# Where the operands of the weight products begin in an SBUF partition: from 704 bytes past a multiple of 2 KB to the multiple itself

## Chip, cores, metric

One Trainium2 chip, one core of it. The metric is device time in microseconds (us) of one execution; the kernel before takes 1866.35 us, the median of 3 runs (1865.23 to 1867.15).

## What is computed

One decoder layer on 256 tokens of width 2048, everything in float32:

```python
h = x + 0.5 * swiglu(rms_norm(x), w_gate1, w_up1, w_down1)        # 2048 -> 5632 -> 2048
proj = rms_norm(h) @ w_in                                          # q, k, v, forget logits; q, k, v
o = concat([rms_norm(forgetting_attention(...)),                   # 16 heads of 64, causal
            rms_norm(sliding_window_sink_attention(...))])         # 16 query, 4 key heads, window 128
h = h + o @ w_out
y = h + 0.5 * swiglu(rms_norm(h), w_gate2, w_up2, w_down2)
```

Nearly all of the arithmetic is in the eight weight matrices. Each is read once, 336 MB in all.

## The kernel before

**Products.** A weight product multiplies activations (stationary operand, 128 rows by 128 tokens) with a block of weights (moving operand, 128 rows by 512 columns) and adds into one PSUM bank. To keep float32 accuracy each operand is split into a high part of type float32r and the remainder, and `mm3` (L178 to L181) issues three matmuls for each product: high by high (L179), high by low weights (L180), low activations by high weights (L181). Every matmul loads its own stationary operand first.

**Loop.** `token_major` (L184) runs over the contraction in steps of two 128-row groups (`kg`, with `k` 0 and 1 in it) and over the two halves of 128 tokens. For each `kg` it calls `weights` (L90): SP issues the transfer of a tile `raw` of 128 by 1024 float32 (L93), ScalarE rounds it to `whi` (L94), VectorE subtracts to get `wlo` (L95). Each of the three has four buffers. `k` 0 takes the first `width` columns of `whi` and `wlo`, `k` 1 the next `width` (L195). `width` is 512, but 388 for the projection `ws` of the sliding-window part and the forget logits, whose tile is 776 wide.

**Stages.** FFN1 gate and up (11 blocks of 512 columns each, stationary operand `u`), FFN1 down (`hT`, 44 groups of 128, of the tile `hT1`), the 388-wide projection (`u`), attention together with the projections `wf` (`u`), the output projection (first half `u` buffers, second half `oTf`), FFN2 gate and up (`u`), FFN2 down (`hT2`). Between the products TensorE transposes results for the next stage (L213). PE, ACT and DVE work through lists whose order is fixed when the program is built.

**Places in SBUF.** Tiles of a pool lie one behind the other in a partition, in steps of 32 bytes, pool behind pool in the order `keep`, `wp`, `sp`, and then `f1`, `mix` and `f2` in the same place one after the other. `cst` (3712 bytes), `vec` (904) and `pos` (8) come first, then `h`, `u0` and `u1` (16,384 each) and the twelve weight tiles (4096 each), all sizes multiples of 2048; so all of these begin at the same remainder. The program built from the kernel has these starts, as remainders of the start in the partition by 2048 bytes:

| operand | role | start mod 2048 | bytes read by one matmul |
|---|---|---|---|
| `whi`, `wlo`, 512 wide, k 0 and 1 | moving | 704 | 2048 |
| `whi`, `wlo`, 388 wide, k 0 / k 1 | moving | 704 / 208 | 1552 |
| `u0`, `u1` | stationary | 704 (+ 0, 512, 1024, 1536 for part and token half) | 512 |
| `hT1`, `hT2` | stationary | 1184 (+ the same) | 512 |
| `oTf0`, `oTf1` | stationary | 640 (+ the same) | 512 |

A 512-wide moving operand so always runs across a multiple of 2 KB (704 + 2048 bytes). Of the 388-wide ones that of k 0 does (704 + 1552 = 2256), and that of k 1 doesn't (208 + 1552 = 1760). Of the stationary ones one in four does.

## Time and profile before

| | |
|---|---|
| median of 3 runs | 1866.35 us |
| the profiled execution, its own time | 1865.22 us |
| its span in the trace, first to last instruction | 1863.0 us |
| TensorE busy | 1834.8 us (98%) |
| weight loads busy (PEld) | 1513.8 us (81%) |
| VectorE / ScalarE busy | 986.2 us (53%) / 843.4 us (45%) |
| DMA, read from HBM | 336 MB, 182 GB/s over the span |
| mean granted TensorE clock | 0.995 |

Matmuls overlap in the trace: a 512-wide one is shown with 0.39 us while the next starts 0.23 us after it. What a stream of them costs is therefore read from the distance of their starts (called pace below), never from the duration. The timeline gives starts to 10 ns; a pace is taken over many starts.

### The profile page before, as it was taken

To read this page: it belongs to the slowest core of one execution; us is meant where nothing else is said; L and a number is where in the kernel's file an instruction comes from. 1 tells how busy PE (TensorE), PEld (TensorE's weight loads), DVE (VectorE), ACT (ScalarE), POOL (GpSimd) and SP (SyncE) were. 2 spreads that over 40 slices of the span, in tenths; PEclk is the share of its full clock that TensorE was granted. 3 is DMA by queue.
4 is the path that set the end of the run, shared out by engine and by line. 5 is a ranking of instruction groups with operands and counts; after the bars stand their busy time and mean duration, and the time that the engine had idled before them with its cause. 6 is when DMAs were issued, how large, how long until landed. Compare 5 with 4: busy or idle time off the path is not lost.

```text
span 1863.0 us, 21805 instructions
## 1 busy us (share of the span) xinstructions
PE 1834.8 (98%) x8396; PEld 1513.8 (81%) x8396; DVE 986.2 (53%) x1194; ACT 843.4 (45%) x1073; POOL 20.9 (1%) x27
## 2 busy tenths in 40 slices
PE   8999999999999999969999999999999999999999
PEld 6888888888888888967888788888888888888887
DVE  6445545454544444666757665454554554444443
ACT  6444444444434443535657554444444444433332
POOL 2000000000000000000000000000000000000000
PEclk9999999999999999989999999999999999999999
DMA  8555555555555555553444355555555555555553
GB/s 301 190 189 191 193 189 188 188 192 192 186 187 181 185 188 175 177 160 104 155 140 146 136 187 186 192 187 187 191 192 188 184 192 190 185 190 199 197 203 113
DMA packets 96440, 339.79 MB, mean 182 GB/s; under 512 B 10832, under 2 KB 10960, under 8 KB 96080
## 3 DMA queue, kind: packets, MB, share of 16 engines
q1 hardware_dynamic: 95040, 336.19, 52.3%
q10 hardware_dynamic: 1296, 2.21, 0.4%
q8 instruction: 65, 1.06, 0.2%
q14 instruction: 39, 0.32, 0.1%
HBM read 336.27 MB, written 2.10 MB: 182 GB/s over the span
## 4 chain that ended last, share of the span: by engine, by line
PE 97%; DMA 1%; DVE 1%; ACT 0%; issue 0%; SPq 0%; DVEq 0%; ACTq 0%
PE acc L179 31%; PE acc L181 31%; PE acc L180 31%; PE sm L213 1%; DMA xc<-in_xT 1%; PE sc L546 1%; PE sm L441 1%; PE sm L447 1%; PE sc L618 1%; PE sm L597 0%; DMA raw<-in_wg 0%; PE sm L448 0%; ACT whi L94 0%; DVE tr L516 0%; DVE qr L517 0%
## 5 line engine op out<-in xcount | busy, mean ns | idle before, releaser
L95 DVE TENSOR_TENSOR wlo<-raw,whi 128x1024 fp32r<-128x1024 f32 (+2 forms) x648 | 778.7, 1203 | 833.9 <-ACT whi L94 833.5
L94 ACT CAST whi<-raw 128x1024 fp32r<-128x1024 f32 (+2 forms) x648 | 667.1, 1031 | 910.3 <-PE acc L181 892.5
L179 PE MATMUL acc<-whi,u 128*128 128x512 f32 (+1 forms) x1792 | 693.3, 388 | 2.7 <-ACT u L152 2.2
L181 PE MATMUL acc<-whi,u 128*128 128x512 f32 (+1 forms) x1792 | 691.5, 387 | 2.5 <-DVE u L153 2.5
L180 PE MATMUL acc<-wlo,u 128*128 128x512 f32 (+1 forms) x1792 | 692.0, 386 | 0.7 <-DVE wlo L95 0.7
L179 PEld LDWEIGHTS acc<-whi,u 128*128 128x128 f32 x1792 | 336.3, 188 | 69.2 <-ACT u L152 2.6
L181 PEld LDWEIGHTS acc<-whi,u 128*128 128x128 f32 x1792 | 336.2, 188 | 68.6 <-DVE u L153 3.4
L180 PEld LDWEIGHTS acc<-wlo,u 128*128 128x128 f32 x1792 | 336.5, 188 | 66.0 <-DVE wlo L95 1.9
L179 PE MATMUL acc<-whi,hT 128*128 128x512 f32 x704 | 278.5, 396 | 0.0
L180 PE MATMUL acc<-wlo,hT 128*128 128x512 f32 x704 | 278.1, 395 | 0.0
L181 PE MATMUL acc<-whi,hT 128*128 128x512 f32 x704 | 278.0, 395 | 0.0
L181 PEld LDWEIGHTS acc<-whi,hT 128*128 128x128 f32 x704 | 131.9, 187 | 32.3
L180 PEld LDWEIGHTS acc<-wlo,hT 128*128 128x128 f32 x704 | 132.0, 187 | 32.1
L179 PEld LDWEIGHTS acc<-whi,hT 128*128 128x128 f32 x704 | 132.0, 187 | 32.0
L419 ACT ACTIVATE s<-s,nm 128x128 f32<-128x128 f32 (+1 forms) x64 | 28.3, 444 | 11.2 <-DVE nm L416 8.5
L222 DVE TENSOR_TENSOR hT<-sm,hT 128x512 fp32r<-128x512 f32 x44 | 28.2, 682 | 0.0
L179 PE MATMUL acc<-whi,oTf 128*128 128x512 f32 x64 | 25.3, 396 | 0.0
L180 PE MATMUL acc<-wlo,oTf 128*128 128x512 f32 x64 | 25.1, 391 | 0.0
L181 PE MATMUL acc<-whi,oTf 128*128 128x512 f32 x64 | 25.0, 391 | 0.0
L221 ACT CAST hT<-sm 128x512 fp32r<-128x512 f32 x44 | 23.5, 587 | 0.0
L213 PEld LDWEIGHTS sm<-cst,s 128*128 128x128 f32 x176 | 20.5, 140 | 2.9
L213 PE MATMUL sm<-cst,s 128*128 128x128 f32 x176 | 22.8, 272 | 0.0
(175 smaller groups left out, 568.2 us busy)
## 6 DMA issues: line engine op xcount, KB each, us to landing
raw<-in_wu SPq DMA_DIRECT2D x176, 512.0 KB, 3.2
raw<-in_wd SPq DMA_DIRECT2D x176, 512.0 KB, 3.2
raw<-in_wg SPq DMA_DIRECT2D x168, 512.0 KB, 3.2
raw<-in_wf SPq DMA_DIRECT2D x48, 512.0 KB, 3.6
raw<-in_wo SPq DMA_DIRECT2D x32, 512.0 KB, 3.5
raw<-in_ws SPq DMA_DIRECT2D x32, 388.0 KB, 3.5
raw<-in_wg SPq DMA_DIRECT2D x16, 256.0 KB, 5.2
xc<-in_xT SPq DMA_DIRECT2D x8, 256.0 KB, 4.9
```

What stands on the lines that cost most here:

```text
L94: nc.scalar.copy(hi, raw)
L95: nc.vector.tensor_tensor(out=lo, in0=raw, in1=hi.bitcast(F32), op=ALU.subtract)
L179: nc.tensor.matmul(o, lhsT=shi, rhs=mhi, start=start, stop=False)
L180: nc.tensor.matmul(o, lhsT=shi, rhs=mlo, start=False, stop=False)
L181: nc.tensor.matmul(o, lhsT=slo, rhs=mhi, start=False, stop=stop)
L213: nc.tensor.transpose(bt[:, j * SEQ + t * P : j * SEQ + (t + 1) * P], src[:, t, m], ident)
L221: nc.scalar.copy(hs[:, :, 0, :], v)
L222: nc.vector.tensor_tensor(out=hs[:, :, 1, :], in0=v, in1=hs[:, :, 0, :].bitcast(F32), op=ALU.subtract)
L419: nc.scalar.activation(s[:, j, :], s[:, j, :], AF.Exp, bias=nm[:, i, j : j + 1], accum_out=den[:, i, j : j + 1],)
L441: nc.tensor.transpose(bt[:, j * P : (j + 1) * P], src[:, j, :], ident)
L447: nc.tensor.matmul(bo[rows, c0 : c0 + SEQ], lhsT=vals(0, j), rhs=p0[:, j, :], start=True, stop=False)
L546: nc.tensor.matmul(o_, lhsT=qk[aa][:, j, blk * P : (blk + 1) * P], rhs=qk[aa][:, 4 + half, 0:nk], start=True, stop=True,)
```

## The change

Only places change. `vec` is widened to 1024 bytes and a filler `pad` of 1248 bytes is put behind `pos`, so that `h`, the `u` buffers and the weight tiles begin at multiples of 2048. A filler `sppad` of 1568 bytes makes the pool `sp` end at such a multiple too, so that `hT1` begins at one; a filler of 128 bytes in the pool `f2` puts `hT2` 128 bytes past one. `pf` and `nsink` are widened to 128 bytes each, which puts `oTf0` and `oTf1` at 1664 past one (13 times 128). The 388-wide tiles are loaded as two blocks with a stride of 512 columns, so that k 1 begins at a multiple too; transfer, cast and subtraction of these 32 tiles work on a pattern of 2 by 388 for it.

| operand | start mod 2048 before | after |
|---|---|---|
| `whi`, `wlo`, 512 wide | 704 | 0 |
| `whi`, `wlo`, 388 wide, k 0 / k 1 | 704 / 208 | 0 / 0 |
| `u0`, `u1` | 704 | 0 |
| `hT1` | 1184 | 0 |
| `hT2` | 1184 | 128 |
| `oTf0`, `oTf1` | 640 | 1664 |

No moving operand crosses a multiple of 2 KB any more. No instruction is added, taken away or moved: on each of the five engines the built programs have the same operations in the same order with the same waits; the 32 transfers, casts and subtractions of the 388-wide tiles differ in their pattern alone.

```diff
@@ -89,16 +89,24 @@
 
     def weights(src, tiles=None, at=0):
 
-        raw, hi, lo = (t[:, at : at + src.shape[1]] for t in tiles or weight_tiles())
+        tiles = tiles or weight_tiles()
+        if src.shape[1] % 512:
+            n = src.shape[1] // 2
+            raw, hi, lo = (t.rearrange("p (k n) -> p k n", k=2)[:, :, :n] for t in tiles)
+            src = src.rearrange("p (k n) -> p k n", k=2)
+        else:
+            raw, hi, lo = (t[:, at : at + src.shape[1]] for t in tiles)
         nc.sync.dma_start(raw, src)
         nc.scalar.copy(hi, raw)
         nc.vector.tensor_tensor(out=lo, in0=raw, in1=hi.bitcast(F32), op=ALU.subtract)
-        return hi, lo
+        return tiles[1:]
 
 
     cst = keep.tile([P, C_END], F32, name="cst")
-    vec = keep.tile([P, V_END], F32, name="vec")
+    vec = keep.tile([P, 256], F32, name="vec")
     pos = keep.tile([P, NT], I32, name="pos")
+
+    keep.tile([P, 312], F32, name="pad")
 
     h = keep.tile([P, NT, D], F32, name="h")
     ident = cst[:, C_ID : C_ID + P]
@@ -107,7 +115,7 @@
     m_swa = cst[:, C_MSK : C_MSK + SEQ]
     m_fox = cst[:, C_MSK + SEQ : C_MSK + 2 * SEQ]
     m_caus = m_fox[:, P:SEQ]
-    nc.scalar.dma_start(vec, a["vec"])
+    nc.scalar.dma_start(vec[:, :V_END], a["vec"])
 
     def half_u(i):
         return keep.tile([P, 8, 2, SEQ], F32R, tag="u%d" % i, name="u%d" % i, bufs=1)
@@ -192,7 +200,7 @@
             hi, lo = parts
             for k in range(2):
                 kk = kg * 2 + k
-                m = slice(k * width, (k + 1) * width)
+                m = slice(k * 512, k * 512 + width)
                 for t in range(NT):
                     ts_ = slice(t * P, (t + 1) * P)
                     mm3(
@@ -280,6 +288,7 @@
 
 
     sp = ctx.enter_context(tc.tile_pool(name="sp", bufs=1))
+    sp.tile([P, 392], F32, name="sppad")
     u1 = new_u()
     ss1 = sp.tile([P, 2, SEQ], F32, tag="ss", name="ss1")
     with tc.tile_pool(name="f1", bufs=1) as fp:
@@ -324,7 +333,7 @@
 
 
         n2 = NT * 32
-        pf = ap_.tile([P, NT], F32, name="pf")
+        pf = ap_.tile([P, 32], F32, name="pf")[:, :NT]
         nc.vector.tensor_copy(pf, pos)
         ang = ap_.tile([P, NT, 32], F32, name="ang")
         invf = cst[:, C_INVF : C_INVF + 32]
@@ -384,7 +393,7 @@
 
         tq = rope_tables("tq", V_SQ)
         tk = rope_tables("tk", V_SK)
-        nsink = ap_.tile([P, NH], F32, name="nsink")
+        nsink = ap_.tile([P, 32], F32, name="nsink")[:, :NH]
         nc.vector.tensor_scalar_mul(nsink, vec[:, V_SINK : V_SINK + NH], -1.0)
 
 
@@ -671,6 +680,7 @@
 
     rm2 = rstd_blocks(ss2, "rm")
     with tc.tile_pool(name="f2", bufs=1) as fp:
+        fp.tile([P, 32], F32, name="fpad")
         hT = fp.tile([P, KF, 2, SEQ], F32R, name="hT2")
         then = gate_up(fp, u2, rm2, hT, a["wg2"], a["wu2"])
         y = out.rearrange("(t p) d -> p t d", p=P)
```

## Rows read from the trace of the kernel before

**Rows 1.** The page: busy time by engine; chain that ended last, by engine and line.

```profile
PE 1834.8 (98%) x8396; PEld 1513.8 (81%) x8396; DVE 986.2 (53%) x1194; ACT 843.4 (45%) x1073; POOL 20.9 (1%) x27
...
PE 97%; DMA 1%; DVE 1%; ACT 0%; issue 0%; SPq 0%; DVEq 0%; ACTq 0%
```

**Rows 2.** Groups by line and shape (x count; busy us, mean ns; idle before).

```profile
L95 DVE TENSOR_TENSOR wlo<-raw,whi 128x1024 fp32r<-128x1024 f32 x600 | 736.0, 1227 | 806.7 <-ACT whi L94 806.4
L179 PE MATMUL acc<-whi,u 128*128 128x512 f32 x1664 | 649.9, 392 | 2.7 <-ACT u L152 2.2 <-ACT whi L94 0.5
...
L94 ACT CAST whi<-raw 128x1024 fp32r<-128x1024 f32 x600 | 631.0, 1052 | 873.2 <-PE acc L181 865.0 <-ACT sqh L259 3.5 <-DVE rxy L136 2.6
...
L179 PEld LDWEIGHTS acc<-whi,u 128*128 128x128 f32 x1792 | 336.3, 188 | 69.2 <-ACT u L152 2.6 <-ACT whi L94 1.6 <-issue 1.3
...
L179 PE MATMUL acc<-whi,hT 128*128 128x512 f32 x704 | 278.5, 396 | 0.0
...
L179 PE MATMUL acc<-whi,u 128*128 128x388 f32 x128 | 43.5, 340 | 0.0
...
L94 ACT CAST whi<-raw 128x776 fp32r<-128x776 f32 x32 | 26.9, 841 | 31.7 <-PE acc L181 27.0 <-DVE h L250 2.0 <-ACT whi L94 1.0
...
L179 PE MATMUL acc<-whi,oTf 128*128 128x512 f32 x64 | 25.3, 396 | 0.0
```

**Rows 3.** Timeline, PE, one block with `u`: start us, us, what; second matmul, then the last six.

```profile
64.57 0.39 PE L180 MATMUL acc<-wlo,u 128*128 128x512 f32 x1
...
106.54 0.39 PE L179 MATMUL acc<-whi,u 128*128 128x512 f32 x1
106.77 0.39 PE L180 MATMUL acc<-wlo,u 128*128 128x512 f32 x1
106.99 0.39 PE L181 MATMUL acc<-whi,u 128*128 128x512 f32 x1
107.22 0.39 PE L179 MATMUL acc<-whi,u 128*128 128x512 f32 x1
107.45 0.39 PE L180 MATMUL acc<-wlo,u 128*128 128x512 f32 x1
107.67 0.39 PE L181 MATMUL acc<-whi,u 128*128 128x512 f32 x1
```

**Rows 4.** Stretches: us, busy of PE, PEld, DVE, ACT, POOL (x count), PEclk, DMA share, GB/s.

```profile
64.30:107.62 43.32, 43.32 (x193) 35.87 (x192) 22.05 (x20) 18.47 (x20) 0.00 (x0) 1.00 0.55 193
...
1617.88:1858.43 240.55, 240.55 (x1033) 193.28 (x1032) 106.73 (x92) 87.31 (x85) 0.00 (x0) 1.00 0.53 181
...
757.38:820.78 63.40, 63.40 (x361) 63.40 (x360) 39.44 (x76) 33.70 (x47) 0.00 (x0) 1.00 0.64 194
```

**Rows 5.** Timeline, PE, FFN2 down (`hT2`): second matmul, then the last.

```profile
1618.14 0.40 PE L180 MATMUL acc<-wlo,hT 128*128 128x512 f32 x1
...
1858.48 0.39 PE L181 MATMUL acc<-whi,hT 128*128 128x512 f32 x1
```

**Rows 6.** Timeline, PE, output projection with `oTf`: two matmuls, 70 apart.

```profile
1076.18 0.39 PE L180 MATMUL acc<-wlo,oTf 128*128 128x512 f32 x1
...
1092.21 0.39 PE L181 MATMUL acc<-whi,oTf 128*128 128x512 f32 x1
```

**Rows 7.** Timeline, all engines, in the 388-wide projection: products and their weight loads.

```profile
785.32 0.34 PE L181 MATMUL acc<-whi,u 128*128 128x388 f32 x1
785.32 0.19 PEld L179 LDWEIGHTS acc<-whi,u 128*128 128x128 f32 x1
785.49 0.34 PE L179 MATMUL acc<-whi,u 128*128 128x388 f32 x1
785.50 0.19 PEld L180 LDWEIGHTS acc<-wlo,u 128*128 128x128 f32 x1
```

**Rows 8.** Waits, all engines: engine, line, releaser: us in total, times, longest us.

```profile
ACT whi L94 <- PE acc L181: 892.5, 550, 2.8
DVE wlo L95 <- ACT whi L94: 833.5, 599, 4.4
```

## The prediction

> **What bounds the kernel now.** First the page: TensorE is busy for 98% of the span, and the chain that ended last is 97% TensorE [rows 1]. Nothing else is near: VectorE and ScalarE work about half of the time, and what they wait for is TensorE. The cast of a weight tile waits 892.5 us for the matmuls that hold its buffer, and the subtraction waits 833.5 us for the cast [rows 8]. So the time is the number of matmuls times the distance of their starts, and a change of places can only act through that distance.

> The numbers come from the groups by line: L179 has 1664 products of 512 columns with `u`, 704 with `hT`, 64 with `oTf` and 128 of 388 columns, and L180 and L181 have as many [rows 2]. That makes 4992, 2112, 192 and 384 matmuls.

> The paces come from starts. [...] FFN2 down, 1032 matmuls, takes 240.34 us for 1030 steps, 233.3 ns each [rows 4, 5]. With `oTf` 70 steps take 16.03 us, 229.0 ns each [rows 6]. In the 388-wide stage 360 matmuls stand in 63.40 us, 176.1 ns each [rows 4].

> Three paces for the same matmul with the same moving operand: what differs by the program's table is where the stationary operand begins (704, 1184 and 640). [...] A load shows 188 ns [rows 2] and has 226.8 ns or more. In the `hT` stretch VectorE is busy for 44% and DMA for 0.53, in the `u` stretch for 51% and 0.55 [rows 4]: the slower stretch has less company.

> [...]

> **The change part by part.**

> *`hT1` and `hT2`, from 1184 to 0 and 128.* Before, they are the only stationary operands that start off the weights' own remainder by 480 bytes; that difference, or 1184 itself (a multiple of 32 bytes, where 704 is one of 64 and 640 one of 128), is what their pace goes with. After, `hT1` stands to the weights as `u` does now (no difference), `hT2` at 128. The nearest row for both is the pace of `u`: 2112 x (233.3 - 226.8) = -13.7 us, of which each FFN has half, 6.9. [...] It is on the path in full: the matmuls stand back to back.

> *`oTf`, from 640 to 1664, now 384 bytes below the next multiple.* 192 x (229.0 - 226.8) = -0.4 us; bounds +0.8 (192 x 4.3, the pace of `hT`) and -3.0 (192 x 15.7).

> *`u` and the 512-wide weights, both from 704 to 0.* Their distance stays nothing. What goes is the crossing of the multiple of 2 KB by the moving operand, and no row shows a 512-wide float32r product without it. [...] I take 0. One in four stationary operands of `u` crosses such a multiple too, the one for L181 of the first token half, loaded while L180 runs; the starts of six matmuls in a row are 0.22 to 0.23 us apart all the same [rows 3]. A crossing by itself so shows no price on that side. The moving side stays open, and is the first rival.

> *The 388-wide products.* Their two halves are the one place where a moving operand crosses (k 0) and doesn't (k 1). They can't tell, since there the loads set the pace: loads are busy for 63.40 of 63.40 us [rows 4], each begins with the matmul before it (785.32, 785.50) and its own matmul starts 0.17 us later, before the 0.19 us of the load are shown as over [rows 7]. [...] I take 0; bounds -2.5 and +2.5 us (384 x 6.5 ns, the spread between the three 512-wide paces).

> *Transfers, casts and subtractions of the 32 tiles in two blocks of 388.* I cost them at nothing. The cast takes 841 ns of a tile's 12 x 176.1 = 2113 ns and waits 27.0 us in all for TensorE [rows 2]. Without that cover the price would be 32 tiles times what the second block adds; even a tenth of the cast, 84 ns, would be 2.7 us.

> *Sum*: -13.7 - 0.4 = -14.1 us. The profiled execution took 1865.22 us, its span is 1863.0 and 2.2 lie around it, which the change doesn't touch; the median of the runs is 1.13 above it. 1866.35 - 14.1 = **1852.2 us**. What is late next is again TensorE: at 226.8 ns a tile of `hT` weights lasts 2.72 us, against 1.05 for its cast and 1.23 for its subtraction.

> **The rivals.**

> *The moving operand pays for its place, and the change takes that away.* [...] Against it: crossings of stationary operands show nothing. [...]

> *Slower: the same remainder for everything is the bad place.* If weights and stationary operand at one and the same multiple get in each other's way, as `hT` at 1184 now does, the `u` products go to 233.3 ns: 1866.35 + 32.4 + 0.8 = 1900, with `hT` unchanged. It decides from 2.8 ns more for `u` on (14.1 us over 4992 matmuls). Against it: `u` and weights share a remainder already, 704, and have the best pace.

> *Same, by absolute places.* If 0 and 128 act as 640 does, all go to 229.0 ns: 4992 x 2.2 = +11.0, 2112 x -4.3 = -9.1, together +1.9 us, 1868.

> *Same, since places aren't the cause.* The paces belong to the stages (the accumulation's length, the company), and the change moves addresses without acting on what makes them differ: 1866. The stretches' shares above speak against it.

> **How the numbers follow.** Forecast 0.40 (within it `hT2` at 128 may gain nothing, then 1859); moving operand pays 0.27, spread from 1754 to 1845; slower 0.12; same by absolute places 0.09; places not the cause 0.12. About 0.2% (3.7 us) is what a measurement of this kernel can tell from no change. Faster by more: 0.40 + 0.27 = 0.67. Within: 0.09 + 0.12 = 0.21. Slower: 0.12. For 8 in 10 the range leaves out the slower rival (0.12) and the strongest quarter of the moving one (0.07): from 1771 to 1870, the upper end being no change with the bounds of the 388-wide products.

> **What would show it.** Right: in FFN1 and FFN2 down the starts are 226.8 ns apart instead of 233.3, in the gate and up blocks still 226.8, and FFN2 down takes about 6.9 us less. [...] FFN1 and FFN2 down with different paces would mean that 128 bytes matter. Wrong at the root: all paces as before.

## The result and the profile after

The changed kernel takes 1856.66 us, the median of 5 runs (1855.54 to 1857.80), against 1866.35 us. The ratio is 0.995, with a 95% interval from 0.9934 to 0.9966: faster by 9.7 us, between 6 and 12. The forecast was 1852.2 us in a range from 1771 to 1870. One more execution of the kernel before took 10,365 us and one of the kernel with one filler, below, 8835 us; the record does not show why, and the ratios leave both out.

In the rows and the code, `...` stands for lines that are not shown.

The page of the changed kernel, busy time by engine and the chain that ended last, answers to [rows 1]:

```profile
PE 1829.8 (99%) x8396; PEld 1517.3 (82%) x8396; DVE 986.2 (53%) x1194; ACT 844.0 (45%) x1073; POOL 20.6 (1%) x27
...
PE 97%; DVE 1%; DMA 1%; ACT 1%; issue 0%; SPq 0%; ACTq 0%; DVEq 0%
```

TensorE is still the chain, VectorE and ScalarE do what they did. So the paces have to tell. The timeline of the changed kernel, PE alone (start us, us, what): the second and the last matmul of a block with `u`, of FFN1 down with `hT1` between two groups of transposes, of a stretch with `oTf`, and of FFN2 down with `hT2` after its transposes. The matmuls stand at L187 to L189 here.

```profile
64.93 0.40 PE L188 MATMUL acc<-wlo,u 128*128 128x512 f32 x1
...
108.01 0.39 PE L189 MATMUL acc<-whi,u 128*128 128x512 f32 x1
...
509.07 0.40 PE L188 MATMUL acc<-wlo,hT 128*128 128x512 f32 x1
...
568.46 0.39 PE L189 MATMUL acc<-whi,hT 128*128 128x512 f32 x1
...
1069.37 0.40 PE L188 MATMUL acc<-wlo,oTf 128*128 128x512 f32 x1
...
1085.63 0.39 PE L189 MATMUL acc<-whi,oTf 128*128 128x512 f32 x1
...
1611.73 0.39 PE L188 MATMUL acc<-wlo,hT 128*128 128x512 f32 x1
...
1851.08 0.40 PE L189 MATMUL acc<-whi,hT 128*128 128x512 f32 x1
```

| stretch | steps | us | ns a matmul after | before |
|---|---|---|---|---|
| `u` | 190 | 43.08 | 226.7 | 226.8 (43.10 us, [rows 3]) |
| `hT1` | 262 | 59.39 | 226.7 | 233.3 (as FFN2 down, [rows 5]) |
| `oTf` | 70 | 16.26 | 232.3 | 229.0 [rows 6] |
| `hT2` | 1030 | 239.35 | 232.4 | 233.3 [rows 5] |

Four facts stand in it. The moving operands no longer cross a multiple of 2 KB, and the `u` blocks are as long as before. `hT1` has fallen to the pace of `u`. `hT2`, 128 bytes past a multiple, has gained 0.9 ns and not 6.5. `oTf` has become slower. By the paces: 1056 x 6.6 = 7.0 us for `hT1`, 1056 x 0.9 = 1.0 for `hT2`, less 192 x 3.3 = 0.6 for `oTf`, together 7.4 us; the two spans in the trace, 1863.0 and 1855.6, differ by just that, and the products with `u` differ by no more than 0.2 ns each (226.9 and 226.7 in the long blocks). The 9.7 us between the medians are 2.3 more: the profiled execution of the kernel before, 1865.22 us, is the fastest of those beside it, that of the changed kernel, 1857.80 us, the slowest of five. Each kernel's executions scatter by about 1 us either way, and 7.4 lies within the interval; what makes executions of one kernel differ the traces don't tell.

The stretches of the changed kernel (busy of PE, PEld, DVE, ACT, POOL, clock, DMA share, GB/s) answer to [rows 4]:

```profile
1611.50:1851.00 239.50, 239.50 (x1033) 194.23 (x1032) 106.67 (x92) 87.38 (x85) 0.00 (x0) 1.00 0.52 182
750.60:813.90 63.30, 63.30 (x361) 63.30 (x360) 39.34 (x75) 33.61 (x47) 0.00 (x0) 1.00 0.62 195
```

In the 388-wide stage loads fill the whole stretch as before, 63.30 of 63.30 us. Its pace has to be read from starts too, not from the chosen stretches of 63.40 and 63.30 us. The second and the last of its 360 matmuls, in the kernel before and in the changed one:

```profile
757.59 0.34 PE L180 MATMUL acc<-wlo,u 128*128 128x388 f32 x1
...
820.83 0.34 PE L181 MATMUL acc<-whi,u 128*128 128x388 f32 x1
```

```profile
750.74 0.34 PE L188 MATMUL acc<-wlo,u 128*128 128x388 f32 x1
...
813.98 0.34 PE L189 MATMUL acc<-whi,u 128*128 128x388 f32 x1
```

358 steps take 63.24 us in both, 176.6 ns each: the second blocks, now at a multiple, changed nothing. The granted clock is 1.00 in both stretches.

### The profile page after: what moved, and what is told of

It reads as the page before. It is cut to its first block, busy times and chain, and to the rows that moved or that the text cites. A ratio compares the mean times of both kernels' runs of the same rounds, so it can differ in the third digit from the quotient of the medians.

```text
span 1855.6 us, 21805 instructions
## 1 busy us (share of the span) xinstructions
PE 1829.8 (99%) x8396; PEld 1517.3 (82%) x8396; DVE 986.2 (53%) x1194; ACT 844.0 (45%) x1073; POOL 20.6 (1%) x27
## 4 chain that ended last, share of the span: by engine, by line
PE 97%; DVE 1%; DMA 1%; ACT 1%; issue 0%; SPq 0%; ACTq 0%; DVEq 0%
PE acc L187 31%; PE acc L189 31%; PE acc L188 31%; PE sm L221 1%; PE sc L555 1%; PE sm L450 1%; PE sm L456 1%; PE sc L627 1%; DMA raw<-in_wg 0%; DMA xc<-in_xT 0%; PE sm L606 0%; ACT whi L100 0%; PE sm L457 0%; DVE tr L525 0%; DVE qr L526 0%
## 5 line engine op out<-in xcount | busy, mean ns | idle before, releaser
L187 PE MATMUL acc<-whi,u 128*128 128x512 f32 (+1 forms) x1792 | 694.0, 388 | 0.8 <-ACT u L160 0.7
L189 PE MATMUL acc<-whi,u 128*128 128x512 f32 (+1 forms) x1792 | 692.0, 387 | 2.5 <-DVE u L161 2.5
L189 PEld LDWEIGHTS acc<-whi,u 128*128 128x128 f32 x1792 | 336.7, 188 | 68.5 <-DVE u L161 3.5
L187 PEld LDWEIGHTS acc<-whi,u 128*128 128x128 f32 x1792 | 337.0, 188 | 67.8 <-ACT u L160 1.6
L187 PE MATMUL acc<-whi,hT 128*128 128x512 f32 x704 | 276.2, 392 | 0.0
L189 PE MATMUL acc<-whi,hT 128*128 128x512 f32 x704 | 275.8, 392 | 0.0
L189 PEld LDWEIGHTS acc<-whi,hT 128*128 128x128 f32 x704 | 132.4, 188 | 29.3
L187 PEld LDWEIGHTS acc<-whi,hT 128*128 128x128 f32 x704 | 132.4, 188 | 29.0
L187 PE MATMUL acc<-whi,oTf 128*128 128x512 f32 x64 | 25.5, 398 | 0.0
L189 PE MATMUL acc<-whi,oTf 128*128 128x512 f32 x64 | 25.2, 394 | 0.0
```

Source lines behind the costliest of these rows:

```text
L187: nc.tensor.matmul(o, lhsT=shi, rhs=mhi, start=start, stop=False)
L189: nc.tensor.matmul(o, lhsT=slo, rhs=mhi, start=False, stop=stop)
```

## The experiments

The theory after the result: the pace of a matmul goes with the *distance*, the start of its stationary operand minus the start of its moving one, and 0 is the best seen. The rivals: the multiple of 2 KB is what counts; the stationary operand's own place counts; the stage counts.

**Everything at a multiple.** Of the changed kernel `hT2` and `oTf` too are put at a multiple of 2 KB.

```diff
-        pf = ap_.tile([P, 32], F32, name="pf")[:, :NT]
+        pf = ap_.tile([P, 128], F32, name="pf")[:, :NT]
...
-        fp.tile([P, 32], F32, name="fpad")
```

> The changed kernel with hT2 at a multiple of 2 KB instead of 128 bytes past one, and oTf at such a multiple instead of 1664 past one; u, hT1 and the weights stay at multiples. Theory of distance (a product's pace goes with where its stationary operand starts against its moving one, 0 being the best seen): FFN2 down falls from 232.4 to 226.7 ns a matmul, 1056 x 5.7 = 6.0 us, the oTf products from 232.4 to 226.7, 192 x 5.7 = 1.1 us, so 1856.7 - 7.1 = 1849.6 us. Theory of absolute places gives the same. Rival, the slower pace of FFN2 down is that of the last stage and not of the 128 bytes: FFN2 down stays at 232.4 and the time at 1856.7 us.

Measured: 1850.39 us, ratio to the kernel before 0.991 (0.9896 to 0.9923). FFN2 down of this kernel, second and last matmul:

```profile
1610.19 0.40 PE L188 MATMUL acc<-wlo,hT 128*128 128x512 f32 x1
...
1843.67 0.39 PE L189 MATMUL acc<-whi,hT 128*128 128x512 f32 x1
```

233.48 us for 1030 steps are 226.7 ns. So the 128 bytes were the whole reason for the pace of FFN2 down, not the stage; with `oTf` at 226.8 ns too this is the fastest kernel of the study, 6 us below the changed one.

**One filler alone.** The kernel before, with `hT1` and `hT2` moved from 1184 to 704 past a multiple, where `u` and the weights are.

```diff
     sp = ctx.enter_context(tc.tile_pool(name="sp", bufs=1))
+    sp.tile([P, 392], F32, name="sppad")
```

> The kernel before with one edit: a filler of 1568 bytes that moves hT1 and hT2 from 1184 to 704 past a multiple of 2 KB, where u and the weights already are. Nothing begins at such a multiple, and every moving operand still crosses one. oTf goes from 640 to 160. Theory of distance: hT falls from 233.3 to 226.7 ns, 2112 x 6.6 = 13.9 us; oTf, then 480 bytes off the weights by 512 as hT was before, rises from 229.0 to 233.3, 0.8 us; 1866.35 - 13.1 = 1853.2 us. Rival, the multiple of 2 KB itself is what helps: hT stays at 233.3 and the time at 1866 us.

Measured: 1851.86 us, ratio 0.9923 (0.9909 to 0.9936).

```profile
1612.79 0.39 PE L180 MATMUL acc<-wlo,hT 128*128 128x512 f32 x1
...
1846.30 0.39 PE L181 MATMUL acc<-whi,hT 128*128 128x512 f32 x1
```

233.51 us for 1030 steps: 226.7 ns with nothing at a multiple and every moving operand across one. `oTf`, now 160 past a multiple and so 32 bytes short of a multiple of 256 from the weights, went to 233.3 ns (70 steps) as expected. The multiple of 2 KB is not what helps; one line gives more than the whole change (1851.86 us against 1856.66).

**Everything 128 bytes further.** The changed kernel with a larger first filler and without that of `f2`.

```diff
-    keep.tile([P, 312], F32, name="pad")
+    keep.tile([P, 344], F32, name="pad")
...
-        fp.tile([P, 32], F32, name="fpad")
```

> The changed kernel with everything 128 bytes further: weights, u, hT1 and hT2 all begin 128 past a multiple of 2 KB, so that they stand to each other as u and the weights do now, but all moving operands cross a multiple again. oTf keeps its distance of 128 from the weights by 512. Theory of distance: u, hT1 and hT2 at 226.7 ns, oTf at 232.4 as in the changed kernel; 1856.7 - 6.0 = 1850.7 us. Theory of absolute places of the stationary operand (128 is a bad one, as hT2 shows at 232.4): u and hT at 232.4, 1856.7 + (4992 + 1056) x 5.7 ns = 1891 us.

Measured: 1852.43 us, ratio 0.9923 (0.991 to 0.9937).

```profile
508.10 0.40 PE L188 MATMUL acc<-wlo,hT 128*128 128x512 f32 x1
...
567.50 0.40 PE L189 MATMUL acc<-whi,hT 128*128 128x512 f32 x1
...
1612.35 0.39 PE L188 MATMUL acc<-wlo,hT 128*128 128x512 f32 x1
...
1845.86 0.39 PE L189 MATMUL acc<-whi,hT 128*128 128x512 f32 x1
```

59.40 us for 262 steps and 233.51 for 1030, 226.7 ns in both. `hT2` is at the same 128 as in the changed kernel, where it cost 232.4; only the weights have moved along. The stationary operand's place by itself doesn't count, the distance does.

**More distances.** With the weights at a multiple, `hT1` and `hT2` are put at two distances in each of four kernels. The first three change fillers in the pools `f1` and `f2` (in 4-byte elements; shown for 64 and 256), the last takes slices of larger tiles, since pools step by 32 bytes. Each of these kernels, and of those after them, ran once; since executions of one kernel differ by 2 us, their times are good to that; their paces are means over hundreds of starts.

```diff
+        fp.tile([P, 16], F32, name="fpad1")
         hT = fp.tile([P, KF, 2, SEQ], F32R, name="hT1")
...
-        fp.tile([P, 32], F32, name="fpad")
+        fp.tile([P, 64], F32, name="fpad")
         hT = fp.tile([P, KF, 2, SEQ], F32R, name="hT2")
```

> The changed kernel with hT1 64 and hT2 256 bytes past a multiple of 2 KB, weights at a multiple: two more distances. Theory of distance: neither is at 226.7 ns; hT1 near the 229.0 that a distance of -64 showed (oTf in the kernel before), hT2 between 229 and 233.3; about 1856.7 + 2.4 = 1859 us. Theory that only a remainder by 64 bytes counts: 64 and 256 are as good as 0, both stages at 226.7, 1850.7 us.

Measured: 1857.05 us. FFN1 and FFN2 down:

```profile
508.04 0.40 PE L188 MATMUL acc<-wlo,hT 128*128 128x512 f32 x1
...
569.17 0.39 PE L189 MATMUL acc<-whi,hT 128*128 128x512 f32 x1
...
1616.86 0.40 PE L188 MATMUL acc<-wlo,hT 128*128 128x512 f32 x1
...
1850.34 0.39 PE L189 MATMUL acc<-whi,hT 128*128 128x512 f32 x1
```

At 64 it is 61.13 us for 262 steps, 233.3 ns; at 256 233.48 for 1030, 226.7 ns, as at 0. Both numbers missed the expectation: +64 is not like -64, and 256 is as good as none. The form the theory took from here: the distance counts by its remainder by 256, so that -64 is 192 and 480 is 224.

> The changed kernel with hT1 192 and hT2 320 bytes past a multiple of 2 KB. Theory that the distance counts by 256 bytes: hT1 as at -64 before, 229.0 ns; hT2 as at 64, 233.3 ns; time 1856.7 + 1056 x (229.0 - 226.7 + 233.3 - 232.4) = 1860 us. Rival, that it counts by 512 bytes or that farther is better: 320 is not as 64, hT2 then nearer to 226.7 ns.

Measured: 1859.18 us.

```profile
507.62 0.39 PE L188 MATMUL acc<-wlo,hT 128*128 128x512 f32 x1
...
567.60 0.39 PE L189 MATMUL acc<-whi,hT 128*128 128x512 f32 x1
...
1612.14 0.40 PE L188 MATMUL acc<-wlo,hT 128*128 128x512 f32 x1
...
1852.47 0.40 PE L189 MATMUL acc<-whi,hT 128*128 128x512 f32 x1
```

228.9 ns at 192 (59.98 us for 262 steps) and 233.3 at 320 (240.33 for 1030): both as said, 192 like the -64 of `oTf` before [rows 6], 320 like 64.

> The changed kernel with hT1 160 and hT2 384 bytes past a multiple of 2 KB. Theory that the distance counts by 256 bytes: hT2 as at 128, 232.4 ns, so that FFN2 down is as in the changed kernel; hT1 at a new distance, between 229 and 233.4 ns; time 1859 to 1864 us. Rival, by 512 bytes: hT2 differs from 232.4.

Measured: 1865.05 us; `hT2` at 384 has 232.4 ns, like 128, and `hT1` at 160 has 233.3. The paces hold; the time is 1 us over the range.

> The changed kernel with hT1 32 and hT2 96 bytes past a multiple of 2 KB: two new distances from the weights. Seen so far (distance by 256 bytes: pace): 0 and 256: 226.7 ns; 64: 233.3; 128: 232.4; 192 (as -64): 229.0; 224 (as 480): 233.3. Theory that the distance counts by 256 bytes and every one but 0 costs something: both stages between 229 and 233.4 ns, FFN downs together 486 us or so, time 1854 to 1860 us. Rival, that there is a distance better than 0: one of the stages below 226.7.

Measured: 1867.08 us; 233.3 ns at 32 and 234.3 at 96 (241.31 us for 1030 steps), the slowest of all:

```profile
1619.07 0.40 PE L188 MATMUL acc<-wlo,hT 128*128 128x512 f32 x1
...
1860.38 0.39 PE L189 MATMUL acc<-whi,hT 128*128 128x512 f32 x1
```

The second misses the upper bound by 0.9 ns and the time by 7 us. The expected time was too low for its own paces: with the measured ones 1856.7 + 1056 x (6.6 + 1.9) is 1865.7. So bad distances can eat up what the change gave.

> The changed kernel with hT1 16 and hT2 240 bytes past a multiple of 2 KB, two distances that are no multiples of 32. Theory that every distance but a multiple of 256 costs: both between 229 and 234.3 ns, 1859 to 1865 us. Rival, that a small distance is as good as none: hT1 at 226.7 ns.

Measured: 1857.91 us. At 240 FFN2 down has 228.3 ns (235.19 us for 1030 steps), under the 229 expected. At 16 FFN1 down has two paces in one and the same execution. Each of its four blocks of 512 columns begins without a pause, and 24 matmuls later transposes stand between; so a stretch from transposes to transposes runs into the next block. The first three stretches, with the first matmul of the second block (564.48) and of the third (626.79), then FFN2 down:

```profile
510.30 0.39 PE L188 MATMUL acc<-wlo,hT 128*128 128x512 f32 x1
...
564.48 0.39 PE L187 MATMUL acc<-whi,hT 128*128 128x512 f32 x1
...
569.69 0.39 PE L189 MATMUL acc<-whi,hT 128*128 128x512 f32 x1
...
571.02 0.40 PE L188 MATMUL acc<-wlo,hT 128*128 128x512 f32 x1
...
626.79 0.40 PE L187 MATMUL acc<-whi,hT 128*128 128x512 f32 x1
...
632.16 0.40 PE L189 MATMUL acc<-whi,hT 128*128 128x512 f32 x1
...
633.50 0.39 PE L188 MATMUL acc<-wlo,hT 128*128 128x512 f32 x1
...
692.89 0.39 PE L189 MATMUL acc<-whi,hT 128*128 128x512 f32 x1
...
1616.02 0.39 PE L188 MATMUL acc<-wlo,hT 128*128 128x512 f32 x1
...
1851.21 0.40 PE L189 MATMUL acc<-whi,hT 128*128 128x512 f32 x1
```

262 steps take 59.39 us, then 61.14, then 59.39: 226.7, 233.4 and 226.7 ns, with the same distance; the rest of the fourth block runs at 233.3 again. The change comes at the transposes and not where a block begins: the first 24 matmuls of the second block, 564.48 to 569.69, still run at the fast pace (5.21 us for 23 steps), those of the third, 626.79 to 632.16, at the slow one (5.37 us). So it isn't the block's PSUM bank or the weight buffer it starts with. Both the theory (over 229) and its rival (226.7) are half wrong here. The distance alone doesn't set the pace at 16: here it changed between 226.7 and 233.4 ns where the stream starts again after transposes, and why stays open.

All distances seen, by their remainder by 256:

| distance | ns a matmul | where |
|---|---|---|
| 0 | 226.7 to 226.9 | `u` in long blocks without a wait; `hT1` after; `hT2` all at a multiple, all 128 further, one filler, at 256; `oTf` all at a multiple |
| 16 | 226.7 or 233.4 | `hT1` |
| 32 | 233.3 | `hT1` |
| 64 | 233.3 | `hT1`; `hT2` at 320 |
| 96 | 234.3 | `hT2` |
| 128 | 232.2 to 232.4 | `hT2`, `oTf` after; `hT2` at 384 |
| 160 | 233.3 | `hT1` |
| 192 | 228.9 to 229.0 | `hT1`; `oTf` before |
| 224 | 233.3 | `hT2` before; `oTf` with one filler |
| 240 | 228.3 | `hT2` |

A rival that the traces can settle is that the stationary operand gets in the way of VectorE's or ScalarE's accesses to SBUF, and not of the moving operand. In FFN2 down of the kernel before (distance 224) a step during which VectorE is busy throughout takes 233.5 ns and one during which it is idle 233.4; with ScalarE it is 233.4 and 233.7. So neither engine is behind the slow pace there. Whether the transfers into SBUF have a part in it was not tried.

**Does the load's length count?** The natural reason would be that the next stationary operand is read from SBUF while the moving one streams, since a load begins with the matmul before its own (within 0.01 us, [rows 7]); then a shorter load should make the matmul that it runs under faster. One kernel halves a load in the FFN down stages, with `hT1` at 0 and `hT2` at 64; half of the correction by the low activations is left out there.

```diff
...
+        n = slo.shape[1] // 2 if half else slo.shape[1]
         nc.tensor.matmul(o, lhsT=shi, rhs=mhi, start=start, stop=False)
-        nc.tensor.matmul(o, lhsT=shi, rhs=mlo, start=False, stop=False)
-        nc.tensor.matmul(o, lhsT=slo, rhs=mhi, start=False, stop=stop)
+        nc.tensor.matmul(o[:n], lhsT=slo[:, :n], rhs=mhi, start=False, stop=False)
+        nc.tensor.matmul(o, lhsT=shi, rhs=mlo, start=False, stop=stop)
...
```

> The changed kernel with hT1 at distance 0 and hT2 at distance 64, and in the two FFN down stages the matmul of low activations by high weights takes only 64 of the 128 stationary columns (half of that correction is left out) and stands second of the three. Its weight load is then half as long, and it runs during the first matmul. [...]

Measured: 1861.87 us. The loads by shape, and the two stages:

```profile
L188 PEld LDWEIGHTS acc<-whi,hT 128*128 128x128 f32 x704 | 132.2, 188 | 30.7
L189 PEld LDWEIGHTS acc<-whi,hT 128*64 128x64 f32 x704 | 94.5, 134 | 30.7
...
507.57 0.40 PE L189 MATMUL acc<-whi,hT 128*64 128x512 f32 x1
...
567.77 0.40 PE L190 MATMUL acc<-wlo,hT 128*128 128x512 f32 x1
...
1614.81 0.40 PE L189 MATMUL acc<-whi,hT 128*64 128x512 f32 x1
...
1855.13 0.40 PE L190 MATMUL acc<-wlo,hT 128*128 128x512 f32 x1
```

The load is shorter, 134 against 188 ns, and nothing is relieved: 60.20 us for 262 steps is 229.8 ns with `hT1`, slower than before, and 240.32 for 1030 is 233.3 with `hT2`, unchanged. The first of the three matmuls, during which the half load runs (one such load begins at 530.09, the matmul at 530.08), takes 228.9 and 233.1 ns from start to start, where the pace at these distances with whole loads is 226.7 and 233.3: 2.2 slower, and 0.2 faster. The control has the same order of the three matmuls with whole loads:

> As the kernel of the half load (hT1 at distance 0, hT2 at 64, the matmul of low activations standing second of the three everywhere), but with all 128 stationary columns: the control for it. Theory that the half load itself made the hT1 stage slower there (229.8 ns instead of 226.7): here hT1 is at 226.7 and hT2 at 233.3 ns, 1857.7 us. Rival, that the order of the three did: hT1 at 229.8, 1861 us.

Measured: 1856.86 us, 226.7 ns with `hT1` (59.40 us for 262 steps) and 233.3 with `hT2`:

```profile
507.47 0.40 PE L189 MATMUL acc<-whi,hT 128*128 128x512 f32 x1
...
566.87 0.39 PE L190 MATMUL acc<-wlo,hT 128*128 128x512 f32 x1
```

So the order isn't what made the first stage slower, by 3.1 ns: it is the half load, or the matmul with 64 stationary columns that comes with it, which no run parts. A price that grows with the length of the load is out at these two distances.

**Which matmul pays?** High and low parts in two tiles: 64 bytes between them and the weights for the low part in FFN1, for the high part in FFN2.

```diff
...
+        hThi = fp.tile([P, KF, SEQ], F32R, name="hThi1")
+        fp.tile([P, 16], F32, name="fpad1")
+        hTlo = fp.tile([P, KF, SEQ], F32R, name="hTlo1")
...
+        hTlo = fp.tile([P, KF, SEQ], F32R, name="hTlo2")
+        fp.tile([P, 16], F32, name="fpad")
+        hThi = fp.tile([P, KF, SEQ], F32R, name="hThi2")
```

> The changed kernel with the high and the low parts of hT in two tiles: in FFN1 the high part at a multiple of 2 KB and the low one 64 bytes past one, in FFN2 the low part at a multiple and the high one 64 past. So of the three matmuls of a product some take a stationary operand at distance 0 from the weights and some one at 64. Theory that a load disturbs the matmul that runs while it loads: in FFN1 the second matmul (the low part is loaded during it) takes 233.3 ns, the first and the third 226.7; in FFN2 the first and the third 233.3, the second 226.7. Rival, that a matmul pays for its own stationary operand: in FFN1 the third is slow, in FFN2 the first and the second. Both give means of 228.9 and 231.1 ns and about 1856.7 + 1056 x (2.2 - 1.3) = 1857.7 us.

Measured: 1861.89 us, 4 us over. Both stages run at 231.1 ns; the second was expected so, the first at 228.9. The rows are FFN1 down, the first 24 matmuls of FFN2 down, which come before its transposes (1610.42 to 1615.78), and the rest of FFN2 down:

```profile
510.26 0.39 PE L196 MATMUL acc<-wlo,hThi 128*128 128x512 f32 x1
...
570.81 0.39 PE L197 MATMUL acc<-whi,hTlo 128*128 128x512 f32 x1
...
1610.42 0.40 PE L195 MATMUL acc<-whi,hThi 128*128 128x512 f32 x1
...
1615.78 0.40 PE L197 MATMUL acc<-whi,hTlo 128*128 128x512 f32 x1
...
1617.13 0.40 PE L196 MATMUL acc<-wlo,hThi 128*128 128x512 f32 x1
...
1855.18 0.39 PE L197 MATMUL acc<-whi,hTlo 128*128 128x512 f32 x1
```

From start to start, over some 350 steps each in the trace, first, second and third take 228.4, 229.2 and 235.7 ns in FFN1 (distances 0, 0, 64) and 226.1, 235.7 and 231.7 in FFN2 (64, 64, 0). In both the slowest step is the one in which a matmul at 64 runs and one at 0 is loaded. Neither theory said so: with the running matmul's own distance FFN2's first would be slow, with that of the loaded one FFN1's third would be fast. And one part in three at 64 costs as much as two in three. But this too depends on more than the places: the first 24 matmuls of FFN2 down, before its transposes (1610.42 to 1615.78, 5.36 us for 23 steps), take 236, 229 and 235 ns, 233.3 in the mean, and the slow steps are the first and the third. So which matmul pays is not shown, and why stays open.

## Why the prediction was right, and where not

*What bounds the kernel*: right. The time of the profiled pair followed the paces, 7.4 us by paces and 7.4 by spans, and no other engine appeared.

*The pace of `u`*: right. The 226.8 ns in both terms of the sum are 43.10 us for 190 steps, from the second to the last matmul of a block [rows 3].

*`hT1`*: right in size. It was taken at the pace of `u`, 6.9 us; the paces say 7.0.

*`hT2`*: the term that was mis-sized. "The nearest row for both is the pace of `u`" priced 128 bytes of distance like none, 6.9 us; measured 1.0. The row that was really near was that of `oTf`, the only other operand off the weights by a small distance, but as the table shows it wouldn't have given the size either: -64 has 229.0 and 128 has 232.4. The case was named inside the forecast, at 1859 us, and so was what would show it, different paces in FFN1 and FFN2 down. By the paces that were built the time is 1866.35 - 7.4, which is 1859; that the median came out at 1856.7, nearer to 1852.2, lies within the scatter of the executions and is luck, no merit of the sum. By paces half of the forecast gain was there.

*`oTf`*: wrong in sign, +0.6 us instead of -0.4, within its bounds. The change took it from a distance of -64 to 128, from 229.0 to 232.3 ns. No run shows the 15.7 ns in its bound of -3.0: the lowest pace `oTf` had is 226.8 ns, at distance 0, 2.2 below 229.0.

*`u` and the crossing*: right, and shown twice. 226.8 ns with all crossings, 226.7 without any (226.9 and 226.7 in most long blocks of the two kernels); and 226.7 for `hT` with crossings (one filler alone). The conclusion from the stationary crossings, that a crossing has no price, held for the moving side.

*The 388-wide stage, and transfers and casts in blocks*: right at nothing, 176.6 ns before and after. The prediction's 176.1 was misread: it divides a chosen stretch by the number of matmuls, and from start to start it is 176.6. The 2113 ns of a tile become 2119, which changes nothing.

*The rivals*: the moving operand that pays for its place, 0.27, did not come: without a crossing the pace of `u` is 226.7 ns, as good as the 226.8 before. No run shows the paces that its spread from 1754 to 1845 stands for; that spread was the author's estimate, and no 512-wide stage that was measured had a pace below 226.7. It alone made the range 99 us wide, so the place of 1856.7 within it says little. Its lower end is not the stated quarter either: the strongest quarter of 1754 to 1845 ends at 1777, not 1771. The slower rival, whose 32.4 us are 4992 x 6.5, did not come. That absolute places count, 0.09, is refuted by the kernel with everything 128 bytes further. That places aren't the cause at all is refuted by the single filler.

*The two readings left open*, the distance to the weights or the multiple of 32, are decided: it is the distance. At 128 past a multiple `hT2` had 232.4 ns with the weights at 0 and 226.7 with the weights at 128. 1184 was bad (233.3 ns) because the weights stood at 704, and the change helped where it made the distance 0, which the multiple of 2 KB did by the way.

## What to carry to other kernels

Where matmuls stand back to back, take their pace from the starts, stage by stage, and set it beside the places of both operands as built: a stage that is 3% slower than another with the same shapes (233.3 against 226.7 ns here) may only have a tile that starts at another distance from its weights. For float32r products such as these, put stationary and moving tiles a multiple of 256 bytes apart (226.7 ns here, at 0 and at 256), for instance with one filler at the head of a pool; where in the partition they begin was worth nothing here (226.7 ns with both at 0, at 128 and at 704 past a multiple of 2 KB). A price read from one value of a periodic quantity must not be carried to another value: measure the distance that will be built.
